# Four paired slabs in every second group, with a fourth raw buffer, a fifth weight place, and the residual's memory for the summed blocks

## The chip, the cores and the metric

The kernel runs on one core of a Trainium2 chip. The metric is the device time of one execution in microseconds (us). All operands are float32. The core has a tensor engine (PE, whose weight loads are shown as PEld), a vector engine (DVE), a scalar engine (ACT), GpSimd (POOL) and a queue engine (SP). DMAs are issued from SP's, POOL's and ACT's instruction streams and run on 16 shared DMA engines.

## The reference

One encoder layer on 256 rows of width 2048: a mixer block, cross attention to 256 memory rows, then a gated feed-forward with 5632 hidden columns, and a last norm. The change touches the feed-forward alone:

```python
def swiglu(h, w_gate_up, w_down):
    gate, up = jnp.split(h @ w_gate_up, 2, axis=-1)
    return (jax.nn.silu(gate) * up) @ w_down
...
        x = x + mix @ w_out[l]
        x = x + cross_attention(rms_norm(x, norm_g[l, 1]), mem_n, w_xq[l], w_xkv[l], w_xo[l])
        x = x + swiglu(rms_norm(x, norm_g[l, 2]), w_gate_up[l], w_down[l])
    return rms_norm(x, final_norm_g)
```

## The kernel before

**Weights as a stream.** All weights are laid out on the host in the order of use, as slabs of 128 partitions by 2048 columns (16 blocks of 128 by 128, 1024 KB). The class Stream loads a slab into a raw buffer (pool rawp, 3 buffers, L97), and splits it by halves of 1024 columns into a high part, wh, cast by ACT (L135, L147), and a low part, wl = raw - wh, by DVE (L136, L148). A pair of wh and wl is a weight place. There are three places in pool wp and a fourth in a pool called `extra` (wx in the attention, wy in the feed-forward); `_buffers` (L88) takes the fourth for every fourth half. `_fill` (L166) makes halves ahead of PE as far as there are places. A product of two float32 operands is three PE instructions: high times high, high times low, low times high (`part`, L432 to L434).

**The feed-forward.** `gate_up` (L1047) makes the hidden values in 11 groups of 512 columns, each with 512 columns of gate and 512 of up: 16 blocks of the inner dimension for each, 8 slabs a group. The first group is done plainly by `gemm_rows`. The ten others go through `paired_rows` (L463) with a plan of eight letters. N is a plain slab: four pieces of 128 by 512, each multiplied with both halves of the 256 rows, 8 x 3 = 24 PE instructions. S is a paired slab: two blocks of the inner dimension and both column sets are multiplied by the seven-product scheme for 2 x 2 blocks, 7 x 3 = 21 instructions, from sums of weights and sums of activations. The sums of activations are made once by `combine` and kept in the tiles z. The sums of weights are needed for every slab.

**The weights of a paired slab** have four pieces s0 to s3 of 512 columns. `_sums` (L140) makes the four phases that PE takes in order: s1 and s2 as they are (1024 columns), s0 (512), and then two summed blocks of 1024 columns each. In the feed-forward's first product the first summed block comes from DMA: `_load` (L94) loads s3 twice into the two halves of a tile `two` (L101, on SP) and then adds s1 and s2 onto it by an accumulating DMA from POOL (L102). That is begun with the load of the slab before (n // 16 + 1). DVE makes the second summed block by two additions in the raw buffer (L158). PE then waits in turn for wh and wl of each phase.

**After a group** DVE and ACT join the seven partial products (`mixed`, L1064), apply the gate (`gated`, L1073; `upped`, L1079), and `store_turned` (L553) transposes the result and stores it to a DRAM tensor, `hidden`, from POOL. A background generator, `fetch` (L1087), reads it back (L564, on POOL) and splits it into the tiles f for the product `w_down`. `down` (L1138) then does that product in two passes, with paired slabs too, whose weight sums are all made by DVE.

**What sets the order.** A scheduler orders each engine's instructions, by the priority of the program's order; each engine then runs its own list in order. Where `keep_place` (L308) is called, an instruction is tied to the one before it on its engine. Background generators are stepped between products by estimates of the time passed.

**Memory.** The residual rows x lie in the tiles res0 to res3, 128 by 1024 each, read again by `down` (`half`, L810). In the feed-forward, pool fp holds 14 tiles f and 3 tiles z, wy the fourth weight place, tw two tiles `two`, gp the values of the gate and four arrival buffers.

Of the kernel before, what the change touches and what calls it, by code (L numbers as in the profile page):

```python
# [13 lines left out]
F32 = mybir.dt.float32  # L14
F32R = mybir.dt.float32r
# [8 lines left out]
P = 128  # L24
R = 256
# [24 lines left out]
PAIRED = {a + i for a, plan in [(GATE_UP + 8 * j, GROUP) for j in range(10)] + [(DOWN, PASSES[0]), (DOWN + 22, PASSES[1])]  # L50
          for i, x in enumerate(plan) if x == "S"}
SUMMED = {i for i in PAIRED if i < DOWN}

# [18 lines left out]
class Stream:  # L72


    def __init__(self, tc, pools, W, bg):
        self.tc, self.nc, self.W, self.bg = tc, tc.nc, W, bg
        self.rawp, self.wp = pools
        self.order = []
        self.n = self.made = 0
        self.after = []  # L80
        self.halves = []
        self.at = self.phase = 0
        self.raw = None
        self.extra = self.sums = None
        self.places = []
        self.two = []

    def _buffers(self, n, m):  # L88

        pool = self.extra if self.extra and len(self.halves) % 4 == 3 else self.wp  # L90
        at = 48 if any(a <= n < b for a, b in ROWS) else 8
        return (pool.tile([P, 1088], F32R, name=t, tag=t)[:, at:at + m] for t in ("wh", "wl"))

    def _load(self, n):  # L94

        nc = self.nc
        self.raw = self.rawp.tile([P, 2048], F32, name="raw", tag="raw")  # L97
        if n // 16 + 1 in SUMMED:
            W, t = self.W[n // 16 + 1], self.sums.tile([P, 1024], F32, name="two", tag="two")
            for a in (0, 512):  # L100
                nc.sync.dma_start(t[:, a:a + 512], W[:, 1536:2048])  # L101
            nc.gpsimd.dma_start(t, W[:, 512:1536], accum_op=ALU.add)  # L102
            self.two.append(t)
        if n // 16 in SUMMED:
            nc.sync.dma_start(self.raw[:, 0:1536], self.W[n // 16][:, 0:1536])
            return
        for a, b in zip(CUTS[n], CUTS[n][1:]) if n in CUTS else [(0, 1024), (1024, 2048)] if self.after else [(0, 2048)]:
            (nc.scalar if (n, a) == (0, 0) else nc.sync).dma_start(self.raw[:, a:b], self.W[n // 16][:, a:b])
            if self.after:
                self.after.pop(0)()  # L110
# [55 lines left out]
    def _fill(self):  # L166

        ahead = self.at + 1 + min(3 if self.extra else 2, self.n // 16)
        while len(self.halves) < ahead and self.made < NBLK:
            self._half()  # L170

    def _used(self):
# [81 lines left out]
class Block:  # L254
    def __init__(self, ctx, tc, t):
        self.ctx, self.tc, self.nc, self.t = ctx, tc, tc.nc, t
        pool = lambda n, b, **kw: ctx.enter_context(tc.tile_pool(name=n, bufs=b, **kw))
        self.cp = pool("cp", 1)
        self.tp = pool("tp", 11)
        self.rp = pool("rp", 3)  # L260
        self.psG = pool("psG", 4, space=PSUM)
        self.psM = pool("psM", 4, space=PSUM)
        rawp = pool("rawp", 3)
        wp = pool("wp", 3)
        self.bg = Background()
        self.st = Stream(tc, (rawp, wp), t["W"], self.bg)
        self.kept = itertools.count()
        self.run()

# [193 lines left out]
    def paired_rows(self, w, cols, slots, sums, plan, mixed, first, ready=None, late=0, before=None, swap=False):  # L463
# [23 lines left out]
        for i, kind in enumerate(plan):  # L487
            if before:
                before(i)
            if kind == "S":  # L490
                ks, z = next(todo)
# [75 lines left out]
    def run(self):  # L567
# [20 lines left out]
        self.ff = self.outside("hidden", FT)  # L588
        self.gk = [nc.dram_tensor(f"state{i}", (R, P), F32, kind="Internal").ap() for i in range(4)]
        self.vd = nc.dram_tensor("values", (P, 8 * 512), F32, kind="Internal").ap()  # L590
        def load(src, k, n):
# [16 lines left out]
        nc.scalar.copy(self.identr, self.ident)  # L608
        with self.tc.tile_pool(name="wx", bufs=1) as st.extra:
            self.attention(self.mixers())  # L610
# [256 lines left out]
    def attention(self, ps):  # L867
        tc, nc, act, st = self.tc, self.nc, self.act, self.st
        with tc.tile_pool(name="atp", bufs=1) as atp, tc.tile_pool(name="kp", bufs=1) as kp, \
# [109 lines left out]
            self.add_rows(1, 2, self.gemm_rows("w_xo", [1024], o)[0])  # L979
            late.append(self.bg.add(self.arrive(self.xf[1], 2, self.tmp, self.put3, FAR), go=True))  # L980
            st.extra = None
            self.add_rows(1, 3, self.gemm_rows("w_xo", [1536], o)[0])
            for g in late[:2]:
                self.bg.drain(g)
# [44 lines left out]
    def mlp(self):  # L1029
        tc, nc, act = self.tc, self.nc, self.act  # L1030
        with tc.tile_pool(name="fp", bufs=1) as fp:
            self.gap(fp, 192)
            f = [fp.tile([P, 512], F32R, name=f"f{i}") for i in range(14)]
            z = [fp.tile([P, 1024], F32R, name=f"z{i}") for i in range(3)]
            f = act[4:12] + f + [z[i // 2][:, i % 2 * 512:i % 2 * 512 + 512] for i in range(6)] + self.h3
            with tc.tile_pool(name="wy", bufs=1) as self.st.extra:
                self.gap(self.st.extra, 64)
                with tc.tile_pool(name="tw", bufs=2) as self.st.sums, tc.tile_pool(name="gp", bufs=1) as gp:
                    self.gate_up(gp, f, z)
# [7 lines left out]
    def gate_up(self, gp, f, z):  # L1047
# [65 lines left out]

        arrival = lambda: gp.tile([P, R], F32, name="ar", tag="ar", bufs=4)
# [9 lines left out]
        comb = self.bg.add(combined())  # L1124
        ps = self.gemm_rows("w_gate_up", [0, DFF], self.h3,
                            parts=[(range(8), [0]), (range(8, 12), [0]), (range(12), [1]), (range(12, 16), [0]), (range(12, 16), [1])],
                            before=lambda n: n in (1, 3) and self.bg.drain(self.late if n == 1 else last))
        self.bg.drain(col)
        gate(ps[0])
        up(0, ps[1])  # L1130
        early = self.bg.add(fetch(0, FT - 22, 3, 2.0, 15))
        self.bg.drain(comb)
        for j in range(1, DFF // 512):
            upped(j, self.paired_rows("w_gate_up", [j * 512, DFF + j * 512], self.h3, sums, GROUP, mixed, gated, swap=j % 2 == 0)[0])
        self.bg.drain(early)
        self.fetch = self.bg.add(fetch(FT - 22, FT, 6, SOON))

    def down(self, f, sp):  # L1138
# [54 lines left out]
        for i, plan in enumerate(PASSES):  # L1193
# [5 lines left out]
            def before(j):  # L1199
                while plan[j] == "S" and len(made) <= plan[:j].count("S"):  # L1200
                    self.bg.step(next(e for e in self.bg.q if e[0] is g))
                if late and j == len(plan) - 2:
                    st.extra = None

# [686 lines left out]
```

## Time and profile before

| what | us |
|---|---|
| median of 3 runs | 1439.03 |
| lowest and highest run | 1435.91, 1439.53 |
| the profiled execution | 1434.72 |
| its span, first to last instruction | 1432.9 |
| PE busy | 1423.0 |
| DVE busy | 1145.7 |
| ACT busy | 815.8 |

The page of the profile shows one execution: busy time of each engine, the span in 40 slices, the DMA queues, the chain of work that ended last, and groups of instructions by source line, operation and tiles (output <- input), with count, busy time, mean time of one, and idle time before with what ended it. Other views are tables of stages, lists of who waited for whom, and instructions in order of time, where "x3" joins three that follow each other. A PE instruction is shown longer than its pitch, since they overlap.

The ten paired groups run from 783 to 1197 us after the first instruction, 41.4 us each; before them lie the mixer, the attention and the first, plain group, behind them `w_down` and the last norm.

### The profile page before, as it was taken

The page shows a single profiled execution, that of the slowest core. Times are in us where ns is not written, and L with a number is a line of the kernel's source. Part 1 is how long each engine was busy: PE and PEld are TensorE (multiplying, and loading weights), DVE is VectorE, ACT ScalarE, POOL GpSimd, SP SyncE. Part 2 cuts the span into 40 slices and gives each one's busy share as a digit, 9 for nine tenths or more (in the row PEclk, how much of TensorE's full clock was granted, in tenths as well). Part 3 has the DMA queues.
Part 4 walks back from the last instruction along what each step waited for, and adds up shares of the span by engine and source line. Part 5 has one row for each costly group of instructions (what it writes and reads, how often), then busy time and mean ns, then how long its engine had stood idle before and what let it go on. Part 6 is the DMA issues. An engine that isn't in the chain of part 4 may idle for free.

```text
span 1432.9 us, 18653 instructions
## 1 busy us (share of the span) xinstructions
PE 1423.0 (99%) x6589; PEld 1181.4 (82%) x6589; DVE 1145.7 (80%) x1738; ACT 815.8 (57%) x1183; POOL 234.6 (16%) x306
## 2 busy tenths in 40 slices
PE   9999999999999999999999999999999999999997
PEld 8888888888888888888888888888888888788886
DVE  6667868777877767777677888889888888989997
ACT  7556565446745555556455556555555556655655
POOL 0000100013212223531430121122011002000000
PEclk9999999999999999999999999999999999999999
DMA  9877554456667787865986989899999887665554
GB/s 350 299 291 247 205 202 166 171 172 224 198 199 232 235 271 246 275 201 171 287 242 207 283 280 289 275 275 285 294 293 289 264 265 227 217 231 180 193 219 147
DMA packets 73038, 343.80 MB, mean 240 GB/s; under 512 B 10957, under 2 KB 12654, under 8 KB 45168
## 3 DMA queue, kind: packets, MB, share of 16 engines
q1 hardware_dynamic: 54848, 288.98, 57.6%
q0 software_dynamic: 17664, 52.97, 15.6%
q8 instruction: 51, 0.84, 0.2%
q10 hardware_dynamic: 432, 0.66, 0.1%
q14 instruction: 43, 0.35, 0.1%
HBM read 322.12 MB, written 20.45 MB: 239 GB/s over the span
## 4 chain that ended last, share of the span: by engine, by line
PE 98%; DVE 1%; DMA 0%; ACT 0%; issue 0%; SPq 0%; ACTq 0%
PE pg L432 22%; PE pg L433 22%; PE pg L434 22%; PE pm L432 7%; PE pm L434 7%; PE pm L433 7%; PE pg L380 4%; PE pg L381 2%; PE pm L1344 1%; PE pm L1022 1%; PE pm L993 1%; PE pm L1753 0%; DMA raw<-in_W 0%; DVE res L282 0%; PE pm L994 0%; PE pm L1518 0%
## 5 line engine op out<-in xcount | busy, mean ns | idle before, releaser
L136 DVE TENSOR_TENSOR wl<-raw,wh 128x1024 fp32r<-128x1024 f32 (+1 forms) x413 | 494.1, 1211 | 167.6 <-ACT wh L135 164.8
L135 ACT CAST wh<-raw 128x1024 fp32r<-128x1024 f32 (+1 forms) x413 | 424.7, 1043 | 282.9 <-PE pg L434 188.3
L432 PE MATMUL pg<-wh,act 128*128 128x512 f32 (+1 forms) x1191 | 465.5, 391 | 0.0
L433 PE MATMUL pg<-wl,act 128*128 128x512 f32 (+1 forms) x1191 | 463.9, 389 | 0.1
L434 PE MATMUL pg<-wh,act 128*128 128x512 f32 (+1 forms) x1191 | 463.8, 390 | 0.0
L432 PEld LDWEIGHTS pg<-wh,act 128*128 128x128 f32 x1191 | 224.0, 188 | 47.9 <-issue 1.5
L434 PEld LDWEIGHTS pg<-wh,act 128*128 128x128 f32 x1191 | 223.9, 188 | 47.5 <-DVE act L282 0.6
L433 PEld LDWEIGHTS pg<-wl,act 128*128 128x128 f32 x1191 | 224.0, 188 | 46.5 <-DVE wl L136 1.2
L147 ACT CAST wh<-raw 128x1024 fp32r<-128x1024 f32 (+1 forms) x150 | 137.4, 921 | 149.6 <-PE pg L434 53.8
L148 DVE TENSOR_TENSOR wl<-raw,wh 128x1024 fp32r<-128x1024 f32 (+1 forms) x150 | 155.9, 1060 | 52.8 <-ACT wh L147 52.6
L433 PE MATMUL pm<-wl,act 128*128 128x512 f32 x309 | 120.3, 389 | 0.1
L432 PE MATMUL pm<-wh,act 128*128 128x512 f32 x309 | 120.2, 389 | 0.0
L434 PE MATMUL pm<-wh,act 128*128 128x512 f32 x309 | 120.2, 389 | 0.0
L380 PE MATMUL pg<-act,wh 128*128 128x512 f32 x256 | 90.5, 395 | 0.0
L381 PE MATMUL pg<-act,wl 128*128 128x256 f32 x256 | 71.8, 280 | 0.0
L433 PEld LDWEIGHTS pm<-wl,act 128*128 128x128 f32 x309 | 58.0, 188 | 12.3 <-DVE wl L136 0.4
L434 PEld LDWEIGHTS pm<-wh,act 128*128 128x128 f32 x309 | 58.0, 188 | 12.1
L432 PEld LDWEIGHTS pm<-wh,act 128*128 128x128 f32 x309 | 58.0, 188 | 12.0
L102 POOL DMA_DIRECT2D two<-in_W x30 | 26.6, 885 | 237.6 <-DMA two<-in_W 106.4
L158 DVE TENSOR_TENSOR raw<-raw 128x512 f32<-128x512 f32 x90 | 61.8, 687 | 1.2
L147 ACT CAST wh<-two 128x1024 fp32r<-128x1024 f32 x30 | 31.5, 1051 | 52.0 <-PE pg L434 27.0
L380 PEld LDWEIGHTS pg<-act,wh 128*128 128x128 f32 x256 | 48.1, 188 | 10.5
(375 smaller groups left out, 1819.3 us busy)
## 6 DMA issues: line engine op xcount, KB each, us to landing
raw<-in_W SPq DMA_DIRECT2D x216, 1024.0 KB, 5.6
raw<-in_W SPq DMA_DIRECT2D x30, 768.0 KB, 6.3
two<-in_W SPq DMA_DIRECT2D x60, 256.0 KB, 4.8
two<-in_W POOLq DMA_DIRECT2D x30, 512.0 KB, 9.0
raw<-in_W SPq DMA_DIRECT2D x11, 512.0 KB, 7.1
hidden<-g POOLq DMA_DIRECT2D x22, 256.0 KB, 3.8
tmp<-hidden POOLq DMA_DIRECT2D x44, 128.0 KB, 6.0
features<-tmp POOLq DMA_DIRECT2D x32, 128.0 KB, 5.2
```

The lines of the kernel that those rows point to most:

```text
L102: nc.gpsimd.dma_start(t, W[:, 512:1536], accum_op=ALU.add)
L135: nc.scalar.copy(wh[:, a:b], r[:, a:b])
L136: nc.vector.tensor_tensor(out=wl[:, a:b], in0=r[:, a:b], in1=wh[:, a:b].bitcast(F32), op=ALU.subtract)
L147: nc.scalar.copy(wh, src)
L148: nc.vector.tensor_tensor(out=wl, in0=src, in1=wh.bitcast(F32), op=ALU.subtract)
L158: nc.vector.tensor_tensor(out=out, in0=a, in1=b, op=ALU.add)
L380: self.nc.tensor.matmul(p[:, :], wh, slot[:, :], start=start, stop=False)
L381: self.nc.tensor.matmul(p[:, 0:R], wl, slot[:, 0:R], start=False, stop=stop)
L432: self.nc.tensor.matmul(p, hi, wh, start=start, stop=False)
L433: self.nc.tensor.matmul(p, hi, wl, start=False, stop=False)
L434: self.nc.tensor.matmul(p, lo, wh, start=False, stop=stop)
L993: nc.tensor.matmul(p[:, :], q[d][:, r * P:(r + 1) * P], kt[d][:, :], start=d == 0, stop=False)
```

## The change

- **Plan of the groups.** `GROUP = "NNSNSNSN"` becomes two plans by turns, `"NSSNSSNN"` and `"NSNSNSNN"`: four paired slabs in groups 1, 3, 5, 7, 9, in two pairs that follow each other directly, and three in groups 2, 4, 6, 8, 10. There are 35 paired slabs in place of 30.
- **Summed blocks.** s3 is loaded once, on SP, two slabs ahead; ACT copies it into the other half of the tile (new line 118), tied to its place in ACT's order; then POOL adds s1 and s2 by an accumulating DMA. The tiles are res0 to res3, in turn, in place of two tiles `two`.
- **Residual.** Since res is overwritten, `leave` stores each res tile to a DRAM tensor, `residual`, from SP, as soon as it is final, and after the last group four DMAs on SP read them back.
- **Places.** A ring of places replaces `extra`: the place that was used longest ago is next. In the paired groups there are five (wp's three, wy, and a new one, wz, in the memory that `two` had) until slab 5 of group 10, then four.
- **Raw buffers.** A fourth, in a pool rawx, opened when the four arrival buffers have been given up, until the same slab.
- **Tiles.** f has 12 of its own tiles and z has 4. The two values of the hidden rows that would go into the fourth z wait until group 10.

```diff
-GROUP = "NNSNSNSN"
+GROUPS = "NSSNSSNN", "NSNSNSNN"
...
+AHEAD = (-2, -2)
+
+SUMS = [{GATE_UP + 8 * j + i + a: GATE_UP + 8 * j + i for j in range(10) for i, x in enumerate(GROUPS[j % len(GROUPS)]) if x == "S"}
+        for a in AHEAD]
...
     def _buffers(self, n, m):
 
-        pool = self.extra if self.extra and len(self.halves) % 4 == 3 else self.wp
+        slot = min(self.ring, key=lambda x: x[1])
+        assert slot[1] < self.at or slot[1] < 0
+        pool, slot[1] = slot[0], len(self.halves)
...
-        self.raw = self.rawp.tile([P, 2048], F32, name="raw", tag="raw")
-        if n // 16 + 1 in SUMMED:
-            W, t = self.W[n // 16 + 1], self.sums.tile([P, 1024], F32, name="two", tag="two")
-            for a in (0, 512):
-                nc.sync.dma_start(t[:, a:a + 512], W[:, 1536:2048])
-            nc.gpsimd.dma_start(t, W[:, 512:1536], accum_op=ALU.add)
+        slot = min(self.raws, key=lambda x: x[1])
+        slot[1] = n
+        self.raw = slot[0].tile([P, 2048], F32, name="raw", tag="raw")
+        if n // 16 in SUMS[0]:
+            t = self.sums[0]
+            self.sums.append(self.sums.pop(0))
+            nc.sync.dma_start(t[:, 0:512], self.W[SUMS[0][n // 16]][:, 1536:2048])
+            self.begun.append(t)
+        if n // 16 in SUMS[1]:
+            t = self.begun.pop(0)
+            mark = len(nc.cur_bb.bb.instructions)
+            nc.scalar.copy(t[:, 512:1024], t[:, 0:512])
+            self.keep(mark)
+            nc.gpsimd.dma_start(t, self.W[SUMS[1][n // 16]][:, 512:1536], accum_op=ALU.add)
             self.two.append(t)
...
-        ahead = self.at + 1 + min(3 if self.extra else 2, self.n // 16)
+        ahead = self.at + 1 + min(len(self.ring) - 1, self.n // 16)
...
+    def whole(self, c):
+        return self.res[c].rearrange("p k r -> p (k r)")
+
+    def leave(self, c):
+        self.nc.sync.dma_start(self.rd[:, c * 1024:(c + 1) * 1024], self.whole(c))
...
-            f = [fp.tile([P, 512], F32R, name=f"f{i}") for i in range(14)]
-            z = [fp.tile([P, 1024], F32R, name=f"z{i}") for i in range(3)]
+            f = [fp.tile([P, 512], F32R, name=f"f{i}") for i in range(12)]
+            z = [fp.tile([P, 1024], F32R, name=f"z{i}") for i in range(4)]
...
+                    while k0 == 0 and k - ahead >= 20 and "free" not in box:
+                        yield
...
-        sums = [((2 * i, 2 * i + 1), z[i]) for i in range(GROUP.count("S"))]
+        sums = [((2 * i, 2 * i + 1), z[(i + 1) % 4]) for i in range(4)]
...
+        def before(n):
+            if n == 1:
+                self.st.lend(self.wz)
+                self.st.sums = list(whole)
...
+            if n == 3:
+                self.leave(3)
...
+        arp.close()
+        more = ExitStack()
+        rx = more.enter_context(self.tc.tile_pool(name="rawx", bufs=1))
+        self.st.raws.append([rx, -1])
...
         for j in range(1, DFF // 512):
-            upped(j, self.paired_rows("w_gate_up", [j * 512, DFF + j * 512], self.h3, sums, GROUP, mixed, gated, swap=j % 2 == 0)[0])
+            plan = GROUPS[(j - 1) % len(GROUPS)]
+            if j == 10:
+                box["free"] = True
+            upped(j, self.paired_rows("w_gate_up", [j * 512, DFF + j * 512], self.h3, sums[:8 - plan.count("N")], plan, mixed, gated,
+                                      before=lambda i: (j, i) == (10, 5) and self.st.back(self.wz, rx), swap=j % 2 == 0)[0])
+        more.close()
+        for c, x in enumerate(whole):
+            nc.sync.dma_start(x, self.rd[:, c * 1024:(c + 1) * 1024])
```

More of the change, by code (lines that the diff above doesn't have):

```diff
@@ L166, in _fill, with lend, back @@
     def _fill(self):
-        ahead = self.at + 1 + min(3 if self.extra else 2, self.n // 16)
+        ahead = self.at + 1 + min(len(self.ring) - 1, self.n // 16)
         while len(self.halves) < ahead and self.made < NBLK:
             self._half()
+    def lend(self, pool):
+        self.ring.append([pool, -1])
+        return pool
+    def back(self, *pools):
+        self.ring = [x for x in self.ring if x[0] not in pools]
+        self.raws = [x for x in self.raws if x[0] not in pools]
     def _used(self):
@@ L267, in __init__ @@
         self.kept = itertools.count()
+        self.st.keep = self.keep_place
         self.run()
@@ L608, in run @@
         nc.scalar.copy(self.identr, self.ident)
[L609 removed]
+        with self.tc.tile_pool(name="wx", bufs=1) as self.wx:
+            st.lend(self.wx)
             self.attention(self.mixers())
@@ L1121, in combined @@
                 yield from self.combine(z, *(self.h3[k] for k in ks))
-        sums = [((2 * i, 2 * i + 1), z[i]) for i in range(GROUP.count("S"))]
+        sums = [((2 * i, 2 * i + 1), z[(i + 1) % 4]) for i in range(4)]
         comb = self.bg.add(combined())
+        whole = [self.whole(c) for c in range(4)]
+        def before(n):
+            if n == 1:
+                self.st.lend(self.wz)
+                self.st.sums = list(whole)
+            if n in (1, 3):
+                self.bg.drain(self.late if n == 1 else last)
+            if n == 3:
+                self.leave(3)
         ps = self.gemm_rows("w_gate_up", [0, DFF], self.h3,
                             parts=[(range(8), [0]), (range(8, 12), [0]), (range(12), [1]), (range(12, 16), [0]), (range(12, 16), [1])],
-                            before=lambda n: n in (1, 3) and self.bg.drain(self.late if n == 1 else last))
+                            before=before)
         self.bg.drain(col)
+        arp.close()
+        more = ExitStack()
+        rx = more.enter_context(self.tc.tile_pool(name="rawx", bufs=1))
+        self.st.raws.append([rx, -1])
         gate(ps[0])
```

34 lines of the change are left out of this document (22 added, 12 removed).

## The prediction

> **What bounds the kernel now.** I read the page's totals and the chain of waits first, then the table of stages, then who waited for whom on the tensor engine.
>
> ```profile
> span 1432.9 us, 18653 instructions
> PE 1423.0 (99%) x6589; PEld 1181.4 (82%) x6589; DVE 1145.7 (80%) x1738; ACT 815.8 (57%) x1183; POOL 234.6 (16%) x306
> ...
> PE 98%; DVE 1%; DMA 0%; ACT 0%; issue 0%; SPq 0%; ACTq 0%
> ```
>
> ```profile
> 783.00:1197.00 414.00, 414.00 (x1828) 342.87 (x1827) 356.60 (x421) 235.55 (x272) 66.27 (x77) 1.00 0.90 278
> ...
> 907.20:948.60 41.40, 41.40 (x184) 34.31 (x183) 36.51 (x45) 23.86 (x29) 7.76 (x9) 1.00 0.92 283
> ```
>
> ```profile
> PE pm L601 <- DVE eps L602: 1.1, 1, 1.1
> ```
>
> Columns of the second fence: stretch, length, then busy time and instructions of PE, PEld, DVE, ACT, POOL, granted clock, DMA share, GB/s. The ten paired groups of the gate/up product lie in 783 to 1197 us. PE is busy for all 414.00 us of it, at the full granted clock, and in the whole run it waits once, 1.1 us at the start. So every product there is paid at its own pitch, 414.00/1828 = 0.2265 us, and nothing else is paid. Only two things can move the time: fewer products, or a wait that PE has not had. DVE is second: 36.51 of 41.40 us in a typical group.
>
> **Fewer products.** A plain slab is 24 products, a paired one 21. Before there are 3 paired slabs in each of ten groups, 30; after, 4 and 3 by turns, 35. The built program has 15 PE instructions fewer: 15 x 0.2265 = **-3.40 us**. No wait in this stage is left to be removed, so the fourth raw buffer and the fifth weight place cannot gain by themselves; they have to pay for the denser DVE work. This is the largest gain open here, 0.24%.
>
> **More work on DVE.**
>
> ```profile
> L148 DVE TENSOR_TENSOR wl<-raw,wh 128x1024 fp32r<-128x1024 f32 x105 | 128.2, 1221 | 52.8 <-ACT wh L147 52.6
> L158 DVE TENSOR_TENSOR raw<-raw 128x512 f32<-128x512 f32 x90 | 61.8, 687 | 1.2
> L148 DVE TENSOR_TENSOR wl<-raw,wh 128x512 fp32r<-128x512 f32 x45 | 30.7, 683 | 0.0
> ```
>
> A plain slab costs DVE 2 x 1.22 = 2.44 us, a paired one 3 x 1.22 + 0.68 + 2 x 0.69 = 5.72. A group with four then takes 36.51 + 3.28 = 39.8 us of DVE, in 41.40 - 3 x 0.2265 = 40.72 us of PE; a group with three stays at 36.5 of 41.4. So DVE still fits, with 0.9 us over in five groups and 4.9 in the other five. Cost of this by itself: nothing, covered by PE. Without that cover it is rival C.
>
> **Two paired slabs in a row.** Here the change makes a tight place. The program's order for six of the ten pairs (groups 1, 3, 5) is: the cast of the next plain half comes before the fourth cast of the second paired slab, on ACT and on DVE. With five places, that plain half gets the place that the first slab's fourth part leaves. The delays of this chain:
>
> ```profile
> 930.78 0.39 PE L434 MATMUL pm<-wh,act 128*128 128x512 f32 x1
> ...
> 931.20 1.05 ACT L147 CAST wh<-two 128x1024 fp32r<-128x1024 f32 x1 [0.83 <-PE pm L434]
> 933.97 1.05 ACT L147 CAST wh<-raw 128x1024 fp32r<-128x1024 f32 x1 [1.71 <-PE pm L434]
> ...
> 935.40 2.98 ACT L135 CAST wh<-raw 128x1024 fp32r<-128x1024 f32 x3
> ```
>
> ```profile
> 931.63 0.69 DVE L158 TENSOR_TENSOR raw<-two,raw 128x512 f32<-128x512 f32 x1
> ...
> 935.05 1.23 DVE L148 TENSOR_TENSOR wl<-raw,wh 128x1024 fp32r<-128x1024 f32 x1 [0.87 <-ACT wh L147]
> 936.49 3.50 DVE L136 TENSOR_TENSOR wl<-raw,wh 128x1024 fp32r<-128x1024 f32 x3 [0.21 <-ACT wh L135]
> ```
>
> ```profile
> PEld pg L433 <- DVE wl L136: 1.2, 3, 0.4
> ...
> L433 PEld LDWEIGHTS pg<-wl,act 128*128 128x128 f32 x1191 | 224.0, 188 | 46.5 <-DVE wl L136 1.2
> ```
>
> ACT starts 0.03 us after the product that freed its place ends (930.78 + 0.39, then 931.20); DVE 0.03 after the cast (935.02, 935.05). Casts follow each other at (2.98 - 1.05)/2 = 0.965 us on ACT and (3.50 - 1.22)/2 = 1.14 on DVE. Count from the start of the second slab. The first slab's last product began at -0.23 and ends at 0.16; ACT casts the plain half from 0.19 and the fourth part from 1.16; DVE takes the plain half from 1.27 and the fourth part from 2.41 to 3.64. PE reaches the fourth part after 15 products, 3.40; the second of its products, at 3.62, reads the low half, and the row of PEld shows that its weight load is what waits, 0.19 earlier: 3.43. Late by 0.2 us. Bounds: 0.02 (only the product waits) and 0.4 (the longest wait in that row), for six to ten pairs: 0.1 to 4. I take 6 x 0.2 = **+1.2 us**, the worked chain. What is late next is nothing: the plain half is cast already.
>
> **Sums two slabs ahead.** The sum no longer takes two loads on SP and an adding DMA on POOL; it takes one load, a copy on ACT, the adding DMA on POOL. All three now go into residual memory, of which there are four places, so in the order the load stands more than 20 us ahead of the copy. What is new is that POOL's DMA is tied to ACT's place in the weight stream.
>
> ```profile
> L102 POOL DMA_DIRECT2D two<-in_W x30: 850/876/932, 686.0 to 1166.8; - x30
> ...
> DMA to landing us min/median/max: 6.8/9.0/10.9
> ```
>
> ```profile
> 908.72 1.58 POOL L559 DMA_DIRECT2D hidden<-g  x2 [9.45 <-DVE g L557]
> 914.97 3.53 POOL L564 DMA_DIRECT2D tmp<-hidden  x4 [4.67 <-issue]
> 918.65 0.92 POOL L102 DMA_DIRECT2D two<-in_W  x1
> ```
>
> For the second slab of a pair the built program has the adding DMA 53 to 57 products ahead of the slab's first, 12.0 to 12.9 us (one, early in the stage, has more). After landing come DVE's add (0.6), the third cast (1.14, after ACT's 1.05), the second add (0.6), the plain half (1.14) and the fourth cast (1.23): 5.2 us to the weight load due at 3.43. So it must have landed 1.8 us ahead of the slab, that is 10.2 to 11.1 us after its issue. It took 9.0, at most 10.9: in time, by 1 to 2 us. In groups 1, 3 and 5 the second pair's sum stands behind two stores and four loads, and POOL starts it 918.65 - 908.72 = 9.9 us after the first store. That store follows the transposes, some 4 us into the group, so it starts at 13.9 and lands at 20.7 to 24.8, against a due time of 25.1 - 1.8 = 23.3: the median fits, the longest is 1.5 us late. Bounds: 0, and 9 sums x 1.5 = 13. Nearest to the median row: three groups, a third of them late by half of that, **+0.5 us**.
>
> The copy itself is 35 times the 512 cast, on an ACT that has 17.5 us idle in a group:
>
> ```profile
> L147 ACT CAST wh<-raw 128x512 fp32r<-128x512 f32 x45 | 27.9, 621 | 25.8 <-PE pg L434 18.1 <-PE pm L434 7.6
> ```
>
> Behind the copy on ACT wait the next casts; its data were asked for more than 20 us earlier, so it does not hold them. Cost: nothing, 0.6 us in a pair if ACT were tight there; in the chain above it comes after the fourth cast.
>
> **Residual out and back.** Eight DMAs of 512 KB on SP, among the weight loads. Each paired slab loads 256 KB less: 30 x 1792 + 50 x 1024 = 104960 KB before, 35 x 1536 + 45 x 1024 + 4096 = 103936 after, so the DMA engines get no busier than 0.90 over the stage.
>
> ```profile
> SPq L108 <- DVE wl L136: 475.7, 117, 9.8
> ...
> raw<-in_W SPq DMA_DIRECT2D x11, 512.0 KB, 7.1
> ```
>
> SP spends its time waiting for raw buffers, so a DMA put between two loads takes no turn from them unless it waits itself. Residual is wanted next by the first pass of the down product, after 20 slabs. Cost 0, covered by buffers of 3 to 4 slabs; without cover each moves a load by 512 KB at 278 GB/s, 1.9 us, and four of them in the last group would be at most 7.5.
>
> **Sum.** The profiled execution took 1434.72 us: its span, 1432.9, and 1.8 around it. 1434.7 - 3.4 + 1.2 + 0.5 = 1433.0. That execution lies 4.3 us under the median of the three runs, 1439.03; a difference carries over, the level does not. 1439.0 - 1.7 = **1437.3 us**.
>
> **Rivals.**
>
> A: no wait appears. For: the stage shows none at 88% DVE, and the chain's lateness, 0.2, is close to what I can resolve. Against: the order leaves no slack there at all. 1439.0 - 3.4 = 1435.6.
>
> B: the sums land late. Place: POOL's adding DMA for the second slab of each pair. It decides from a landing of 10.7 us; beyond, nine sums stall PE for the excess, and the gain is gone at 10.7 + (3.4 - 1.2)/9 = 10.9. For: 10.9 has been seen, and stores and loads stand before it. Against: the median, and POOL has only 7.76 us of work in a group. At 12 us: 9 x 1.3 + 1.2 - 3.4 = +9.5, 1448.5. The Trainium skill (SBUF — State Buffer, "SBUF: two separate sides") says that DVE operations in a two-port mode keep GpSimd from writing its DMA descriptors. By that rule a DVE that goes from 36.5 to 39.8 us a group lengthens these DMAs. The trace speaks rather against it: POOL's instruction keeps within 850 to 932 ns while DVE is 86% busy.
>
> C: DVE becomes the bound in the five groups of four. It has 4.9 us idle in a group now, much of it waiting for ACT between casts; it decides when more than 0.9 of that stays. If 3 us stay, five groups take 2.1 us longer: 10.5 - 3.4 = +7.1, 1446.1. For: the 52.8 us that row L148 waited for ACT. Against: those waits are for places, and a fifth place shortens them.
>
> D: the change doesn't do what it says, and PE's count stays. The built program excludes it.
>
> **Chances.** Forecast 0.47, A 0.25, B 0.15, C 0.13. A change of 0.3%, 4.3 us, is about what a measurement of this kernel tells from none. Even A is 0.24%, so faster needs A with the runs' scatter (they spread 3.6 us) in its favour: a third of A and a little of the forecast, 0.12. Slower: most of B and C, 0.23. Within: 0.65. Range: A less 3.6 for scatter, 1432, to C, 1446; the likeliest alone, from its bounds of 0.1 to 4 and the scatter, 1434 to 1441.5.
>
> **What would show it.** PE's instructions fall by 15. Groups of four take 40.7 us plus their waits. The forecast's mark is PEld at L433's successor waiting for DVE's wl some 0.2 us, once in each pair of the first groups. B shows as DVE waiting at its add for a DMA into residual, and landings over 10.7; C as DVE at over 39 us in groups that take over 41, with PE waiting for wl throughout. The prediction is wrong if PE's waits in the stage come to over 4 us, or if time moves outside it.

## The result, and the profile after

| | before | after |
|---|---|---|
| median, us | 1437.66 (1435.91 to 1439.53, 4 runs) | 1444.57 (1443.37 to 1444.87, 4 runs) |
| span of the profiled execution, us | 1432.9 | 1441.6 |

The ratio is 1.0046, 95% interval 1.0029 to 1.0064: the kernel is slower by 0.46%. The median lies 6.9 us higher, the span 8.7 us. The prediction had 1.7 us less.

The totals of the page, after:

```profile
span 1441.6 us, 18611 instructions
PE 1424.6 (99%) x6574; PEld 1179.6 (82%) x6574; DVE 1162.3 (81%) x1766; ACT 842.0 (58%) x1230; POOL 239.8 (17%) x311
```

PE has its 15 instructions fewer, 6574 for 6589, and still ends later. Whom PE and then its weight loads waited for, in total, times, longest (us); lines L459 to L461 are the products that were L432 to L434, L153 and L154 the casts and low parts of plain halves (L135 and L136 before), L165 and L166 those of paired slabs (L147 and L148 before):

```profile
PE pg L459 <- ACT wh L153: 3.0, 2, 1.9
PE pm L460 <- DVE wl L166: 2.8, 4, 0.8
PE pg L460 <- DVE wl L154: 1.2, 2, 0.9
PE pm L629 <- DVE eps L630: 1.1, 1, 1.1
PE pm L459 <- ACT wh L165: 0.5, 2, 0.3
```

```profile
PEld pm L460 <- DVE wl L166: 6.6, 10, 1.1
PEld pg L459 <- ACT wh L153: 3.9, 2, 2.3
```

Before, PE waited once. Only the row of L629 is that old one. The others fall into two kinds: waits for plain halves (L153, L154), which are few and long, and waits for the parts of paired slabs (L165, L166). The table of stages (length, then busy time and instructions of PE, PEld, DVE, ACT and POOL, granted clock, DMA share, GB/s) places them. The first line is before, the other two are after:

```profile
737.00:746.00 9.00, 9.00 (x42) 7.44 (x41) 8.64 (x27) 6.35 (x10) 4.63 (x7) 1.00 0.95 310
```

```profile
737.00:746.00 9.00, 7.31 (x24) 5.64 (x25) 9.00 (x16) 5.37 (x9) 2.84 (x4) 0.81 0.54 187
783.00:1197.00 414.00, 410.49 (x1798) 336.44 (x1797) 368.46 (x440) 256.85 (x311) 72.35 (x83) 1.00 0.90 267
```

In the stretch of the ten groups PE runs 1798 instructions in 414 us for 1828 before: 30 x 0.2265 = 6.8 us lost. And the 24 instructions in 9 us from 737 us, for 42 before, are in the first, plain group of the gate and up product. That lies ahead of the stage that the prediction looked at.

For the runs below, one measure is used throughout: wherever the starts of two consecutive products are over 0.29 us apart, the distance less 0.227, added up over a stretch. After has 4.9 us of this from 730 to 760 us, where before has 0.0, and 6.6 us from 783 to 1190 us, where before has 0.0. Less the 3.4 us saved by fewer products that is 4.9 + 6.6 - 3.4 = 8.1 of the 8.7.

**The first loss: a load behind a store, on SP.** SP's own instructions in order of time, in after:

```profile
715.75 0.33 SPq L847 DMA_DIRECT2D residual<-res  x1
721.77 0.33 SPq L113 DMA_DIRECT2D res<-in_W  x1
722.50 18.14 SPq L126 DMA_DIRECT2D raw<-in_W  x4
```

and what SP waited for between 690 and 746 us:

```profile
SPq L113 <- DMA residual<-res: 5.6, 1, 5.6
```

L847 stores the third residual tile; L113 loads the first block of a sum into that tile. The scheduler put this load right behind the store, ten raw loads ahead of its place in the program. It must wait until the store has landed, and SP runs its list in order, so SP issues nothing for 721.77 - 715.75 = 6.0 us. The weight loads stand behind it. ACT, in order of time:

```profile
727.75 1.05 ACT L153 CAST wh<-raw 128x1024 fp32r<-128x1024 f32 x1 [1.67 <-PE pg L461]
735.70 2.94 ACT L153 CAST wh<-raw 128x1024 fp32r<-128x1024 f32 x3 [6.91 <-DMA raw<-in_W]
```

The bracket is the idle time before the cast and what ended it: 6.9 us without weights. The fourth raw buffer is not open yet in this group, and three do not cover it. PE stops for 2.0 and then 1.2 us, and shortly after seven products start 0.427 us apart, not 0.2265, the granted clock of the stretch being 0.81: 7 x 0.2 = 1.4 us more.

**The second loss: four sums that land late.** POOL and DVE at the second slab of the second pair of group 1, after:

```profile
794.17 3.56 POOL L591 DMA_DIRECT2D tmp<-hidden  x4 [4.18 <-issue]
797.69 0.99 POOL L120 DMA_DIRECT2D res<-in_W  x1
814.71 0.87 POOL L120 DMA_DIRECT2D res<-in_W  x1 [16.02 <-ACT res L118]
```

```profile
808.94 0.69 DVE L176 TENSOR_TENSOR raw<-res,raw 128x512 f32<-128x512 f32 x1 [0.90 <-DMA res<-in_W]
```

L120 adds two blocks onto the tile by DMA, L176 is the first instruction of DVE that reads the sum. DVE waits for the landing and starts 808.94 - 797.69 = 11.25 us after the issue. The four loads of L591 stand directly ahead on POOL. All five groups with four paired slabs have such a sum, that of the second slab of their second pair:

| group | issue to landing, us | landed ahead of the slab, us | lost by PE, us |
|---|---|---|---|
| 1 | 11.2 | 0.8 | 1.1 |
| 3 | 11.7 | 0.0 | 1.9 |
| 5 | 11.3 | 0.9 | 1.0 |
| 7 | 12.3 | -0.1 | 1.8 |
| 9 | 9.4 | 2.9 | 0.3 |

By the prediction's chain a sum has to land 1.8 us ahead. The first four miss that by 1.0, 1.8, 0.9 and 1.9 us, which is within 0.1 us what PE loses; the fifth lands in time, and so do the sums of the first pairs. Over all 35 sums, the view of L120 says

```profile
DMA to landing us min/median/max: 5.5/9.9/12.3
```

### The profile page after: what moved, and what is told of

It reads as the page before. It is cut to its first block, busy times and chain, and to the rows that moved or that the text cites. A ratio compares the mean times of both kernels' runs of the same rounds, so it can differ in the third digit from the quotient of the medians.

```text
span 1441.6 us, 18611 instructions
## 1 busy us (share of the span) xinstructions
PE 1424.6 (99%) x6574; PEld 1179.6 (82%) x6574; DVE 1162.3 (81%) x1766; ACT 842.0 (58%) x1230; POOL 239.8 (17%) x311
## 4 chain that ended last, share of the span: by engine, by line
PE 87%; DMA 5%; issue 3%; DVE 2%; ACT 1%; POOL 1%; SPq 0%; ACTq 0%; POOLq 0%
PE pg L459 19%; PE pg L461 19%; PE pg L460 19%; PE pm L460 6%; PE pm L461 6%; PE pm L459 6%; PE pg L407 4%; DMA res<-in_W 3%; PE pg L408 2%; DMA raw<-in_W 1%; PE pm L1409 1%; DMA hidden<-g 1%; POOL tmp L591 1%; PE pm L1060 1%; DVE wl L154 1%
## 5 line engine op out<-in xcount | busy, mean ns | idle before, releaser
L154 DVE TENSOR_TENSOR wl<-raw,wh 128x1024 fp32r<-128x1024 f32 (+1 forms) x403 | 484.4, 1213 | 170.6 <-ACT wh L153 167.3
L153 ACT CAST wh<-raw 128x1024 fp32r<-128x1024 f32 (+1 forms) x403 | 415.7, 1042 | 273.9 <-PE pg L461 185.6
L459 PE MATMUL pg<-wh,act 128*128 128x512 f32 (+1 forms) x1161 | 455.3, 392 | 3.0 <-ACT wh L153 3.0
L460 PE MATMUL pg<-wl,act 128*128 128x512 f32 (+1 forms) x1161 | 453.6, 391 | 1.2 <-DVE wl L154 1.2
L461 PE MATMUL pg<-wh,act 128*128 128x512 f32 (+1 forms) x1161 | 453.5, 391 | 0.0
L459 PEld LDWEIGHTS pg<-wh,act 128*128 128x128 f32 x1161 | 218.8, 188 | 50.0 <-ACT wh L153 3.9
L460 PEld LDWEIGHTS pg<-wl,act 128*128 128x128 f32 x1161 | 218.9, 189 | 46.7 <-DVE wl L154 2.3
L461 PEld LDWEIGHTS pg<-wh,act 128*128 128x128 f32 x1161 | 218.8, 188 | 46.5 <-DVE act L309 0.8
L165 ACT CAST wh<-raw 128x1024 fp32r<-128x1024 f32 (+1 forms) x165 | 150.3, 918 | 144.9 <-DVE raw L176 66.8
L166 DVE TENSOR_TENSOR wl<-raw,wh 128x1024 fp32r<-128x1024 f32 (+1 forms) x165 | 171.8, 1060 | 37.0 <-ACT wh L165 36.8
L460 PE MATMUL pm<-wl,act 128*128 128x512 f32 x314 | 122.4, 390 | 0.1
L461 PE MATMUL pm<-wh,act 128*128 128x512 f32 x314 | 122.3, 390 | 0.0
L459 PE MATMUL pm<-wh,act 128*128 128x512 f32 x314 | 122.3, 389 | 0.0
L120 POOL DMA_DIRECT2D res<-in_W x35 | 31.8, 909 | 236.7 <-ACT res L118 236.5
L460 PEld LDWEIGHTS pm<-wl,act 128*128 128x128 f32 x314 | 59.0, 188 | 12.5 <-DVE wl L154 0.4
L461 PEld LDWEIGHTS pm<-wh,act 128*128 128x128 f32 x314 | 59.0, 188 | 12.2
L459 PEld LDWEIGHTS pm<-wh,act 128*128 128x128 f32 x314 | 59.0, 188 | 12.2
L176 DVE TENSOR_TENSOR raw<-raw 128x512 f32<-128x512 f32 x95 | 65.4, 688 | 0.6
L165 ACT CAST wh<-res 128x1024 fp32r<-128x1024 f32 x35 | 36.9, 1055 | 32.0 <-DMA res<-in_W 12.2
```

The costliest lines, as they stand in the source:

```text
L120: nc.gpsimd.dma_start(t, self.W[SUMS[1][n // 16]][:, 512:1536], accum_op=ALU.add)
L153: nc.scalar.copy(wh[:, a:b], r[:, a:b])
L154: nc.vector.tensor_tensor(out=wl[:, a:b], in0=r[:, a:b], in1=wh[:, a:b].bitcast(F32), op=ALU.subtract)
L165: nc.scalar.copy(wh, src)
L166: nc.vector.tensor_tensor(out=wl, in0=src, in1=wh.bitcast(F32), op=ALU.subtract)
L176: nc.vector.tensor_tensor(out=out, in0=a, in1=b, op=ALU.add)
```

## The experiments

All spans are of one profiled execution; all medians and ratios come with intervals against runs of before on the same chip. The sets of runs were taken on different chips, and the median of before was 1435.9 to 1437.7 us in them.

**One at a time: tying the first loads, and sums three slabs ahead.** Theory: the two losses above are the whole of it, and independent.

```diff
+            mark = len(nc.cur_bb.bb.instructions)
             nc.sync.dma_start(t[:, 0:512], self.W[SUMS[0][n // 16]][:, 1536:2048])
+            if SUMS[0][n // 16] in (GATE_UP + 4, GATE_UP + 5):
+                self.keep(mark)
```

> The third and fourth first loads into residual memory are tied to their place in SP's order, so SP no longer waits at 716 to 722 us for the residual store to land with the weight loads behind it; all else as in the changed kernel. Theory (SP held): PE's wait near 737 us, some 5.3 us with the slow clock behind it, goes; span 1441.6 - 5.3 = 1436.3, ratio to the kernel before 1.0046 - 0.0037 = 1.001. Rival (the DMA engines are full there, share 1.00, and the residual's bytes are the cost): the wait stays within 2 us of what it was, span 1440 or more. The waits in the groups, 5.8 us, stay under both.

```diff
-AHEAD = (-2, -2)
+AHEAD = (-3, -3)
```

> Sums are begun three slabs ahead in place of two; all else as in the changed kernel, the wait near 737 us too. Theory (sums land late): the adding DMA now stands 15 to 27 us ahead of its slab, all land in time, the 5.8 us of PE's waits in the second pairs go down to what the order leaves, at most 1; span 1441.6 - 5.3 = 1436.3, ratio 1.001. Rival (DVE is the bound in groups of four, or the five places are): the waits stay at 4 to 6 us, span 1440 to 1442.

> Both edits. Theory: the two waits are separate and add, span 1441.6 - 5.3 - 5.3 = 1431, which is 2 us under the kernel before, ratio 0.9985 (0.9975 to 0.9995). Rival (one wait only moves to another place when its cover goes, or DVE bounds): span 1435 or more, ratio 1.001 or more.

| | span, us | lost 730 to 760 | lost 783 to 1190 | median, us | ratio to before |
|---|---|---|---|---|---|
| after | 1441.6 | 4.9 | 6.6 | 1444.57 | 1.0046 (1.0029 to 1.0064) |
| loads tied | 1436.0 | 0.0 | 7.5 | 1439.72 | 1.0018 (1.0006 to 1.0029) |
| three ahead | 1435.6 | 4.3 | 1.4 | 1437.79 | 1.0010 (1.0001 to 1.0019) |
| both | 1430.2 | 0.0 | 1.4 | 1432.36 | 0.9970 (0.9959 to 0.9982) |

Each edit takes away its own loss and leaves the other. From the spans, the wait on SP costs 1435.6 - 1430.2 = 5.4 us, the late sums 1436.0 - 1430.2 = 5.8 us, together 11.2 of the 11.4 us between after and the version with both. That version beats before, by 0.3%: 4.4 us by the medians (1436.75 before, in that set), 2.7 us by the spans, since the profiled execution of before is one of its shorter ones. In it SP stores and goes on loading (SP in order of time, both edits):

```profile
714.56 0.33 SPq L850 DMA_DIRECT2D residual<-res  x1
718.07 16.60 SPq L129 DMA_DIRECT2D raw<-in_W  x4
735.93 0.33 SPq L850 DMA_DIRECT2D residual<-res  x1
```

and what is left of waits is, of its stage table and its weight loads:

```profile
783.00:1197.00 414.00, 413.97 (x1820) 340.73 (x1819) 372.14 (x445) 259.27 (x313) 72.04 (x84) 1.00 0.89 269
```

```profile
PEld pm L463 <- DVE wl L169: 2.4, 7, 0.4
```

L463 and L169 are the same products and low parts as L460 and L166. Six of these are the first and second pairs of groups 1, 3 and 5, PE losing 0.18 us at each: the wait for the order of casts that the prediction worked out. Below it is called the order's wait. The seventh, in group 7, costs PE 0.3 us.

**The plan of before with all the rest of the change.** If the rest (buffers, places, memory, copy, due times) cost nothing of its own, this is the span of before plus the wait on SP.

```diff
-GROUPS = "NSSNSSNN", "NSNSNSNN"
+GROUPS = "NNSNSNSN", "NNSNSNSN"
```

> The plan of the kernel before, three paired slabs in each group and never two in a row, with all the rest of the change (places, buffers, residual, sums two slabs ahead). Theory: 15 products more than the changed kernel, +3.4, no wait in the groups, -5.8, the wait near 737 us stays; span 1441.6 + 3.4 - 5.8 = 1439.2, which is 6 over the kernel before, ratio 1.004. Rival (the copies, the longer adding DMAs and the residual traffic cost something in every group, pairs or not): waits in the groups of 3 us or more, span 1442 or more.

The span was 1439.0, the median 1439.55 (ratio 1.0017, 1.0008 to 1.0026). From 730 to 760 us 6.2 us are lost, from 783 to 1190 us 0.0: without a second paired slab following directly, no sum is late enough to stop PE. Then the wait was to be taken out of this version too, with the same tie as above:

> The plan of before (three paired slabs in every group) with all the rest of the change (fourth raw buffer, fifth place, residual's memory for the sums, copy on ACT, sums two slabs ahead), and the first loads into res for the slabs GATE_UP + 4 and + 5 tied to their place in the program. Theory: of the rest of the change only the wait in the plain gate and up part costs time (6.2 us in the run with the three-slab plan), and the fourth pair per second group is worth its 15 products; so the span is 1439.0 - 6.2 = 1432.8 us, that of before within 1 us, and PE has no long gap between 730 and 1190 us. Rival: the rest of the change has a cost or a gain of its own that the ledger did not see: the span lies outside 1431.5 to 1434.5.

The span was 1437.8, the median 1439.50 (ratio 1.0027, 1.0016 to 1.0037). The number lies where the rival put it, but not for the rival's reason. PE still lost 4.2 us from 730 to 760 us, since the wait stood where it was (SP in order of time):

```profile
715.82 0.33 SPq L850 DMA_DIRECT2D residual<-res  x1
721.91 0.33 SPq L114 DMA_DIRECT2D res<-in_W  x1
722.36 17.60 SPq L129 DMA_DIRECT2D raw<-in_W  x4
```

With three slabs in a group the third load into the tiles belongs to slab + 6, and that one had not been tied. It was the edit that missed.

```diff
-            if SUMS[0][n // 16] in (GATE_UP + 4, GATE_UP + 5):
+            if SUMS[0][n // 16] in (GATE_UP + 4, GATE_UP + 6, GATE_UP + 10):
```

> As the run before it with the plan of before, but with the loads into res for GATE_UP + 4, + 6 and + 10 tied to their place: with three slabs in a group the third load into res_102, which came ahead of the raw loads there and waited for the store, belonged to slab + 6, which had not been tied. Theory: the 4.2 us of long gaps between 730 and 760 us and nothing else go away, and the span is 1437.8 - 4.2 = 1433.6 us or up to 1 us less, that of before. Rival: the rest of the change (buffers, places, memory, copy, due times of two slabs) has another cost: span over 1435.

The span was 1433.4, with 0.0 us lost from 730 to 760 and from 783 to 1190; the median was 1434.79, the ratio 0.9993 (0.9984 to 1.0002). So all of the change but the fourth paired slab and that wait costs nothing that the medians show (0.5 us of span). One new wait is seen, on ACT, of the copy for its load, which was issued 6 us before it (ACT in order of time):

```profile
774.79 0.62 ACT L121 COPY res<-res 128x512 f32<-128x512 f32 x1 [5.22 <-DMA res<-in_W]
```

The casts and the gate of the first group stand behind it, and PE loses 1.1 us from 760 to 783 us, where before loses none.

The version with both edits above is 1433.4 - 1430.2 = 3.2 us shorter. That is near the 3.4 us of its 15 products, but the two also differ in what they lose: the former 1.4 us in the pairs, the plan of before 1.1 us ahead of 783 us and 0.8 us more after 1190 us.

**What makes the sums land late.** Theory: the four loads just issued on the same queue. In this run the early loads of `hidden` wait for 14 us more after their store, and are tied there, so that they fall behind the adding DMA.

```diff
                     while len(stored) <= k // 4:
                         yield
+                    while wait and self.bg.now < stored[k // 4] + 14.0:
+                        yield
+                    mark = self.mark()
...
+                    if wait:
+                        self.keep_place(mark)
```

> The changed kernel with one edit: the early loads of the hidden rows are tied to a later place in POOL's order, behind the second pair's adding DMAs in groups 1, 3 and 5; in group 7 they stay ahead of it, and sums are still begun two slabs ahead. Theory (four small-piece loads in flight on POOL's queue lengthen the adding DMA behind them): the landings of these three fall from 11.2 to 11.7 us to 9 to 10, their waits from 1.02, 1.71 and 0.95 us to 0.3 or less, group 7 keeps its 12.3 us and 1.57; span 1441.6 - 3.0 = 1438.6. Rival (the weight loads on SP's queue, or DVE's load, lengthen it): landings stay over 11 us, span 1441 to 1442.

The span was 1444.5, the median 1445.52 (ratio 1.0063, 1.0048 to 1.0079): wrong, and yet the landings went as the theory says. Where the loads had been moved, in groups 1, 3 and 5, the three sums took 8.5, 8.6 and 8.7 us for 11.2, 11.7 and 11.3, and PE lost only the order's wait, 0.2 us, at each. In group 7 four loads remained directly ahead:

```profile
1046.95 3.56 POOL L591 DMA_DIRECT2D tmp<-hidden  x4 [3.50 <-issue]
1050.47 0.99 POOL L120 DMA_DIRECT2D res<-in_W  x1
```

and there the sum took 13.5 us and PE lost 3.4. One kernel shows both cases, so at this place the loads are needed for a late landing. They are not all of it. In before, six sums stand behind four such loads too and took 10.5 to 10.9 us. In the run with the plan of before, and in the one with its third load tied, seven each took 9.2 to 10.9 us. In all of these no earlier sum was in flight. In after, the sum of the pair's first slab was still 1.2 to 2.7 us from landing when the late one was issued, and the loads moved out of the way bring 8.5 to 8.7 us although an earlier sum was in flight there as well. So landings of 11.2 us and more came here with both, loads and an earlier sum. How the two work together stays open: one sum with both, in the run with tied loads, took 9.5 us.

The time that was saved went to a new place: the moved loads of group 1 now come six in a row. POOL, then ACT, in order of time:

```profile
834.47 0.91 POOL L120 DMA_DIRECT2D res<-in_W  x1 [3.71 <-ACT res L118]
835.05 5.65 POOL L591 DMA_DIRECT2D tmp<-hidden  x6
```

```profile
846.46 0.40 ACT L317 CAST act<-tmp 128x256 fp32r<-128x256 f32 x1 [5.99 <-DMA tmp<-hidden]
846.77 1.99 ACT L153 CAST wh<-raw 128x1024 fp32r<-128x1024 f32 x2
```

The first load lands after 11.4 us, its reader on ACT waits 6.0 us for it, and the weight casts stand behind that reader. PE loses 4.7 us at 848.

**Are the fourth raw buffer and the fifth place needed?** From the version with both edits, one is taken away.

```diff
-                self.st.lend(self.wz)
...
-                                      before=lambda i: (j, i) == (10, 5) and self.st.back(self.wz, rx), swap=j % 2 == 0)[0])
+                                      before=lambda i: (j, i) == (10, 5) and self.st.back(rx), swap=j % 2 == 0)[0])
```

> The kernel with both waits taken out (span 1430.2), with four weight places in the paired groups in place of five. Theory by the same chain as in the prediction: with four places the fourth part takes the place that the first slab's last part leaves, cast at 0.2, ready by 3.2 of the 3.43 it has; waits of 0.5 us or less in a pair, span 1430 to 1434. Rival (two paired slabs in a row live on the fifth place): PE waits 0.5 to 2 us in all ten pairs, span 1436 or more.

```diff
-        self.st.raws.append([rx, -1])
...
-                                      before=lambda i: (j, i) == (10, 5) and self.st.back(self.wz, rx), swap=j % 2 == 0)[0])
+                                      before=lambda i: (j, i) == (10, 5) and self.st.back(self.wz), swap=j % 2 == 0)[0])
```

> The kernel with both waits taken out (span 1430.2), with three raw buffers throughout. Theory: raw buffers limit nothing, since the sum no longer hangs on the load of the slab before; span 1430 to 1431.5. Rival (the fourth buffer is what lets weight loads run ahead of the denser casts): ACT waits for raw DMAs and PE for ACT, span 1433 or more.

With four places the span is 1439.4 (median 1440.56, ratio 1.0030, 1.0020 to 1.0039), with three raw buffers 1458.6 (1459.75, ratio 1.0164, 1.0147 to 1.0180). The rivals hold: both are needed, for 9.2 and 28.4 us. What ACT waited for from 783 to 1197 us, first with both edits, then with four places, then with three raw buffers:

```profile
ACT wh L168 <- PE pm L464: 25.8, 23, 2.1
```

```profile
ACT wh L168 <- PE pm L464: 46.4, 34, 2.1
```

```profile
ACT wh L168 <- DMA raw<-in_W: 35.7, 19, 3.3
ACT wh L156 <- DMA raw<-in_W: 24.9, 9, 4.8
```

L168 and L156 are the casts of paired and of plain slabs. With a place fewer ACT waits longer for PE to free one; with a raw buffer fewer the casts wait 35.7 + 24.9 = 60.6 us for weights, a cause that is not among the first nine of that view when there are four.

**More groups of four.** The vector engine's limit, the prediction's rival C, is looked for by putting four pairs into nine groups, then into seven.

```diff
-GROUPS = "NSSNSSNN", "NSNSNSNN"
+GROUPS = ("NSSNSSNN",) * 9 + ("NSNSNSNN",)
```

> The kernel with both waits taken out (span 1430.2), with four paired slabs in groups 1 to 9 and three in group 10: 39 paired slabs, 12 products fewer, -2.7 us. Theory (DVE still fits, 39.8 of 40.7 us a group): four more groups with two pairs each, 8 x 0.2 us more of the order's wait at most, span 1430.2 - 2.7 + 0.8 = 1428.3 (1427.5 to 1429.5). Rival C (DVE is the bound in groups of four once no group of three lies between to catch up): each further group is 1 us or more late, span 1432 or more.

```diff
-GROUPS = "NSSNSSNN", "NSNSNSNN"
+GROUPS = ("NSSNSSNN", "NSSNSSNN", "NSNSNSNN") * 2 + ("NSSNSSNN",) * 3 + ("NSNSNSNN",)
```

> The mended change (sums three slabs ahead, first loads tied) with seven groups of four and three of three, 37 paired slabs in gate and up for 35; 6 products fewer, -1.4 us. Theory: vector engine's postponed work is caught up in the groups of three, and it only runs over when there is none of them until the end, as in the run with nine groups of four; then the six products count and the two more pairs of neighbours cost 0.2 us each, span 1429 to 1430, with no gap over 1 us from 1190 to 1210 us. Rival: what nine groups lost (1443.8 for 1430.2 - 2.7 expected, 16 us) grows with each group of four that has no group of three behind it; half of the four extra ones then lose about 8 us, span 1436 to 1438, with the last loads of tmp from hidden again later than in the mended change (1164 us there, 1196 us with nine).

Nine give a span of 1443.8 (median 1444.90, ratio 1.0060, 1.0047 to 1.0073), seven 1431.9 (1434.36, ratio 0.9988, 0.9979 to 0.9997). With nine, PE loses only 3.1 us from 783 to 1190 us, though DVE is busy for 377.49 of the 414 us, and 13.2 us after 1190. What is left undone in the groups is the work on the hidden values: of the 44 loads of `hidden`, 14 have been issued by 1195 us, for 30 with the change's own plan and 29 with seven groups of four. POOL and ACT with nine groups of four, in order of time:

```profile
1194.62 0.77 POOL L589 DMA_DIRECT2D hidden<-g  x1 [4.63 <-DVE g L587]
1195.63 0.76 POOL L589 DMA_DIRECT2D hidden<-g  x1 [0.25 <-DVE act L312]
1196.38 7.90 POOL L594 DMA_DIRECT2D tmp<-hidden  x9
```

```profile
1200.17 0.40 ACT L320 CAST f<-tmp 128x256 fp32r<-128x256 f32 x1 [4.61 <-DMA tmp<-hidden]
```

These loads, twelve in a row by 1207 us, stand behind the store of the last hidden values, and the next stage's products wait for what is split from them (whom PE waited for):

```profile
PE pg L464 <- DVE f L312: 4.5, 2, 4.1
```

That DVE could not have done this work is not shown: it is idle for 414 - 377.49 = 36.5 us of the stage. The generator that does it is stepped, when the program is built, only while an estimate of DVE's open work is under 0.9 us (`poll` in the class Background), so it may be this rule that holds the work back. With both edits and the change's own plan, the last load ahead of the store and the store itself are (POOL in order of time):

```profile
1164.05 0.90 POOL L594 DMA_DIRECT2D tmp<-hidden  x1 [7.07 <-DVE z L312]
1194.47 1.50 POOL L589 DMA_DIRECT2D hidden<-g  x2 [29.52 <-DVE g L587]
```

The 14 loads that are left in that version begin at 1201.55 us, and PE loses 0.3 us after 1190 us.

Seven groups of four fall between the two expectations. There is no gap of over 1 us from 1190 to 1210 us, as the theory has it. But two loads stand directly behind the last store, at 1195.65 us, and 2.2 us are lost after 1190 us where the change's own plan loses 0.3, most of it near 1233 us; what causes that is not shown. With 0.9 us more lost in the pairs that is 2.8 us against 1.4 gained. The change's own plan by turns is the best of the three.

## Why the prediction was wrong

- **Fewer products, -3.40:** right in the count, 15 instructions fewer. The 3.2 us of span between the versions with and without them agree, though partly by luck, since other losses differ too. That the fourth raw buffer and fifth place gain nothing by themselves is right (1433.4 for 1432.9), and they pay for the denser plan, as stated: 28.4 and 9.2 us more without them.
- **More work on DVE, nothing:** right for four and three by turns. With both edits DVE is busy for 372.14 of 414 us, and PE loses 1.4 us there, all of it at the pairs. With nine groups of four the plan does fail, but not as rival C has it: PE does not wait for wl throughout the groups; background work is postponed to their end, while DVE still has idle time.
- **Two paired slabs in a row, +1.2:** right in place and size. 0.18 us at each of the six pairs of groups 1, 3 and 5, 1.1 in all, and 0.3 at one pair of group 7.
- **Sums two slabs ahead, +0.5:** the mechanism was right, one size was wrong. Issue stood 11.7 to 12.3 us ahead of the slab (12.0 to 12.9 forecast), and the due time of 1.8 us ahead tells the four sums that stopped PE from the fifth, which did not. What failed is the choice "Nearest to the median row: three groups, a third of them late by half of that". (Its own factors give 3 x 1/3 x 0.75 = 0.75, not 0.5.) The median was that of all sums; the ones that matter stand directly behind four loads, with an earlier sum in flight, and those took 11.2 to 12.3 us, not 9.0. The trace of before had half of this: its six sums behind four loads are among its longest, 10.5 to 10.9 us, against the 10.2 to 11.1 that the prediction allows, so "in time, by 1 to 2 us" held for the median alone. Cost 5.8 us, within the bounds of 0 and 13. It is rival B, at four sums and not nine. The rule of the Trainium skill that was named beside it (SBUF — State Buffer, "SBUF: two separate sides") is not what made these sums late: the run with moved loads keeps DVE's work and brings the landings to 8.5 to 8.7 us. The Trainium skill (DMA: Bandwidth & Descriptors, "Two DMAs through the same engine are not ordered") bears on what did: it says that within one queue of one DMA engine descriptors start in order. That agrees with both cases of that run, 8.5 to 8.7 us without the loads ahead and 13.5 us behind them.
- **Residual out and back, cost 0:** this step failed outright. "so a DMA put between two loads takes no turn from them unless it waits itself" is true, and one of them did wait itself, for 5.6 us. The prediction looked at the eight DMAs of the residual, and at the loads into its tiles, but not at how the two meet in SP's order: the load into the third tile directly behind its store. It also took "buffers of 3 to 4 slabs" as cover; in the plain group there are three, and they did not cover 6.0 us without a load issued. Cost 5.4 us, outside the stage of the ten groups. Both things that the prediction had named as making it wrong came about: time moved outside the stage, and PE lost more than 4 us in it, 6.6.
- **The copy on ACT, nothing:** right for the change; the plan of before with it loses 0.0 us in the groups. That its data are asked for more than 20 us earlier does not hold where the load is tied to a later place: there the copy waited 5.2 us, once.

Forecast and measurement so differ by two terms. By the costs that the runs show the span's 8.7 us is -3.4 + 1.1 + 5.4 + 5.8 = 8.9, where the prediction added up -3.4 + 1.2 + 0.5 = -1.7. The measured level, 1444.57, lies in the range of 1432 to 1446 by luck: the upper end was set for rival C, which did not appear.

## What to carry to other kernels

When memory is given a second use, look in the built order of the queue for the first load into it and the last store out of it: a scheduler may bring them together ahead of everything else, and then every load behind waits for the store's landing. Price a DMA that adds by the landings of those that stand behind the same traffic, not by the median of all, and ask what else the new order puts in flight beside it; a slab more of lead cost nothing here and was worth 5.8 us. Extra buffers that gain nothing alone can be what makes a denser plan possible, and a plan that fits while it runs can still leave postponed work to the next stage.

## What the runs showed of the hardware

After a stop PE pays a second time, or not, and the length of the one stop does not tell which. With three raw buffers, a start 2.58 us after the one before was followed by seven products at 0.426 to 0.427 us, one 2.38 us after by none. Two shorter stops close together were enough as well: in after, starts 2.27 and 1.45 us after the one before were followed by seven such products, and in the run with sums three slabs ahead 1.56 and 1.45 us by eight. The half pitch lasted 3.0 us after the stop of 2.58 us, 3.4 us in the run with sums three slabs ahead, and up to 5.1 us in the run with moved loads. The Trainium skill (TensorE: Matmul & The Clock Gate, "Part 1: The HAM clock gate") gives the half rate and a window of about 3.4 us, of which one must be idle; the pitch agrees, but here 2.58 us of stop, and pairs of shorter ones, were enough. DMAs that add took from 5.3 to 13.5 us for the same 512 KB onto the same tiles; the longest stood behind four loads with an earlier sum in flight.
